# Seven matmuls of the identity by itself ahead of the first product of a two-layer encoder trunk

## Chip, cores and metric

One core of a Trainium2 chip runs the whole program. The metric is the device time of one execution in microseconds (us), as the median of several runs.

## What is computed

The reference is a trunk of two post-norm layers over 256 tokens of width 2048, in float32. Each layer is a mixer and a SwiGLU feed-forward block, each followed by a residual layer norm:

```python
for layer in range(DEPTH):
    if layer % 2 == 0:
        y = ab_mixer(x, ab_w_in[j], ab_w_out[j], na_rpb[j], lower_bounds[j], hg_norm_w[j])
    else:
        y = cd_mixer(x, cd_w_in[j], cd_w_out[j], pool_w[j], pool_scale[j], d_q_norm[j], d_k_norm[j], cos, sin)
    x = layer_norm(DN_ALPHA * x + y, ln_mix_g[layer], ln_mix_b[layer])
    f = swiglu(x, ffn_w_gate[layer], ffn_w_up[layer], ffn_w_down[layer])
    x = layer_norm(DN_ALPHA * x + f, ln_ffn_g[layer], ln_ffn_b[layer])
```

The mixer of the first layer begins with one input projection, `proj = x @ w_in`, of 256 x 2048 by 2048 x 8192. Its first 512 columns are the first products of the program.

## The kernel before

The kernel is written with a scheduling layer: the Python code issues tiles and instructions, and a scheduler with a time model of its own sets the order of each engine's queue, except where `tc.keep_in_program_order` pins an instruction.

Every large product is made three times. A float32 operand is split into a rounded part and the rest: `split` (lines 126 to 128) has ScalarE (ACT) copy the source into `hi`, and VectorE (DVE) subtract `hi` from the source into `lo`. `mm3` (line 286) then issues three matmuls into one accumulator: activation rest by weight `hi`, activation `hi` by weight `hi`, activation `hi` by weight rest. In the rows these are `acc<-whi,xTl`, `acc<-whi,xTh` and `acc<-wlo,xTh`. This text calls each such matmul of 128 x 128 by 128 x 512 a product.

Weights come in halves. `load_half` (line 152) loads 256 rows by 512 columns (512 KB) into `raw` through SP's queue and splits them into `whi` and `wlo`, which live in a ring of six buffers in the first mixer. One half serves twelve products: two slices of 128 rows, two tiles of 128 tokens, three matmuls. `mm_chunk` (line 191) takes the eight halves of a chunk of 512 output columns. In the first chunk `load_x` (line 608) also loads and splits the transposed input, four slices at a time for every second half, and the first half and the first input are loaded in two pieces each, so that the first products can start early. Half 0 and half 1 therefore serve products 1 to 24, and half 2 begins with product 25.

The identity matrix `ident` (lines 110 and 111) is made on GpSimd (POOL) at the very start: a memset and an affine select. Its users are the transposes (line 124), the first of them after the first chunk. PSUM tiles come from rings of banks: `acc()` has three, `trp()` (tiles named `tr`) two, `mxp()` three.

At the end of `trunk`, lines 989 to 994 make the tiles for the input and call the first mixer, which issues the first product. Nothing stands for TensorE (PE) ahead of it.

Of the kernel before, what the change touches and what calls it, by code (L numbers as in the profile page):

```python
# [18 lines left out]
P = 128  # L19
# [15 lines left out]
RMS_EPS = 1e-6  # L35
QSCALE = 128 ** -0.5
FILL = -3.0e38


A_Q, A_K, A_V, H_Q, H_FF, H_FB, H_I, H_G = (8 * i for i in range(8))  # L40
# [40 lines left out]
def trunk(ctx: ExitStack, tc: tile.TileContext, a, out):  # L81
    nc = tc.nc
# [16 lines left out]
    def bank(tag, bufs):  # L99
        return banks["pool"].tile([P, NCH], F32, tag=tag, name=tag, bufs=bufs)  # L100

    def side_bank(other=False):
        return bank("ab"[banks["side"] ^ other] + "side", 4)
# [6 lines left out]
    ident = cp.tile([P, P], F32, name="ident")  # L110
# [6 lines left out]
    def trp():  # L117
        return bank("tr", 2) if banks["kind"] == "uses" else side_bank(True)
# [131 lines left out]
    def new_xT():  # L250
        xh = [ap_.tile([P, KT, P], F32R, tag=f"xTh{t}", name=f"xTh{t}") for t in range(NT)]
        xl = [ap_.tile([P, KT, P], F32R, tag=f"xTl{t}", name=f"xTl{t}") for t in range(NT)]
        return xh, xl

    def new_yT():
        yh = ap_.tile([P, 4, T], F32R, tag="yTh", name="yTh", bufs=4)
        yl = ap_.tile([P, 4, T], F32R, tag="yTl", name="yTl", bufs=4)
        return yh, yl
# [348 lines left out]
    def ab_mixer(mp, xT, yT):  # L607
# [196 lines left out]
        def natten(i, outs):  # L804
# [15 lines left out]
            for h in range(2):  # L820
# [6 lines left out]
                for qt in range(NT):  # L827
# [4 lines left out]
                        scale=1.0,  # L832
                        scalar=FILL,
                        op0=add,
# [151 lines left out]
                pool(kind[1], outs)  # L986


    xT = new_xT()
    yT = [new_yT() for _ in range(4)]  # L990
    with tc.tile_pool(name="wab", bufs=1) as wab:
# [41 lines left out]
def constants():  # L1033
# [5 lines left out]
    inside = (col[None, :] >= start[:, None]) & (col[None, :] < start[:, None] + NA_COLS)  # L1039
    colmask = np.tile(np.where(inside, 0.0, FILL), (2, 1)).astype(np.float32)  # L1040
    pos = np.arange(T)
# [83 lines left out]
def build(nc, arrays):  # L1125
    args = {}
    for name, v in arrays.items():
        t = nc.dram_tensor(name, v.shape, mybir.dt.from_np(v.dtype), kind="ExternalInput")
        args[name[3:]] = t.ap()
    out = nc.dram_tensor("out", (T, D), F32, kind="ExternalOutput").ap()  # L1130
    with tile.TileContext(nc, schedule_with_timeline_sim=True) as tc:
        trunk(tc, args, out)
# [11 lines left out]
```

## Time and profile before

| | us |
|---|---|
| median of 3 runs | 2211.68 (2210.59 to 2213.93) |
| the profiled execution's own time | 2208.31 |
| its span, first to last instruction | 2206.5 |
| PE busy | 2176.5 (99% of the span) |
| DVE busy | 1564.1 (71%) |
| ACT busy | 1053.2 (48%) |
| POOL busy | 42.2 (2%) |

The span is the time from the first to the last instruction; 1.8 us of the profiled execution lie outside it. The profiled execution is one of its own, and shorter than the three timed runs. A matmul's shown duration is longer than its share of PE's time, since matmuls are pipelined: the time from one start to the next is what one costs in a dense stretch. A timeline merges equal instructions that follow each other into one row with a count.

### The profile page before, as it was taken

Reading aid. Unit: us, or ns where it says so; the run is one execution under the profiler, and the core shown is the slowest. Engines: PE = TensorE matmul, PEld = TensorE weight load, DVE = VectorE, ACT = ScalarE, POOL = GpSimd, SP = SyncE. Lnnn points to the kernel's source line nnn. Section 1 sums busy time; section 2 is a strip of 40 time slices with the busy share of each in tenths; the row PEclk is TensorE's granted clock in tenths of the full one; section 3 lists DMA queues with packets and bytes.
Section 4 is the critical chain, followed back from the end, with each engine's and each line's share of the span. In section 5 each row is a group of like instructions: output and inputs, shape, how many; then the busy total and the mean of one; then the engine's idle time right before and its main releaser. Section 6 shows DMA issues by size and latency. Waiting matters only on the chain. (4 is left out here: it accounts for less than half of the span.)

```text
span 2206.5 us, 26606 instructions
## 1 busy us (share of the span) xinstructions
PE 2176.5 (99%) x10048; PEld 1806.2 (82%) x10048; DVE 1564.1 (71%) x1960; ACT 1053.2 (48%) x1276; POOL 42.2 (2%) x43
## 2 busy tenths in 40 slices
PE   8999999999999999999999989999999999999997
PEld 7888888888888888888888778888888878888886
DVE  6886688567538787577877676677357886668865
ACT  6445544546435445445544554555344554445442
POOL 0000001000000000000000000000000000000001
PEclk9999999999999999999999999999999999999999
DMA  8555546684636565565557363657456555655573
GB/s 288 163 163 180 171 126 191 210 276 141 231 117 240 178 206 186 190 228 185 189 180 269 127 206 124 213 169 237 154 172 225 184 180 194 212 198 183 179 249 114
DMA packets 112562, 420.64 MB, mean 191 GB/s; under 512 B 13744, under 2 KB 16304, under 8 KB 105520
## 3 DMA queue, kind: packets, MB, share of 16 engines
q1 hardware_dynamic: 112432, 418.93, 57.0%
q8 instruction: 79, 1.29, 0.2%
q14 instruction: 51, 0.42, 0.1%
HBM read 416.78 MB, written 2.10 MB: 190 GB/s over the span
## 5 line engine op out<-in xcount | busy, mean ns | idle before, releaser
L128 DVE TENSOR_TENSOR wlo<-raw,whi 128x1024 fp32r<-128x1024 f32 (+1 forms) x673 | 818.8, 1224 | 435.2 <-ACT whi L127 425.0
L127 ACT CAST whi<-raw 128x1024 fp32r<-128x1024 f32 (+1 forms) x673 | 704.8, 1052 | 827.3 <-PE acc L290 329.0
L290 PE MATMUL acc<-whi,xTl 128*128 128x512 f32 x1056 | 418.3, 397 | 13.2 <-DVE rx L889 6.5
L290 PE MATMUL acc<-whi,xTh 128*128 128x512 f32 x1056 | 415.3, 393 | 0.0
L290 PE MATMUL acc<-wlo,xTh 128*128 128x512 f32 x1056 | 412.7, 393 | 1.0 <-DVE wlo L128 1.0
L290 PEld LDWEIGHTS acc<-whi,xTl 128*128 128x128 f32 x1056 | 199.8, 189 | 54.2 <-ACT whi L127 8.2
L290 PEld LDWEIGHTS acc<-wlo,xTh 128*128 128x128 f32 x1056 | 199.5, 189 | 42.6 <-DVE wlo L128 1.9
L290 PEld LDWEIGHTS acc<-whi,xTh 128*128 128x128 f32 x1056 | 199.8, 189 | 39.2
L290 PE MATMUL acc<-whi,yTl 128*128 128x512 f32 x512 | 200.4, 392 | 0.1
L290 PE MATMUL acc<-whi,yTh 128*128 128x512 f32 x512 | 199.5, 390 | 0.0
L290 PE MATMUL acc<-wlo,yTh 128*128 128x512 f32 x512 | 197.7, 390 | 0.0
L290 PE MATMUL aside<-whi,xTl 128*128 128x512 f32 x336 | 131.2, 390 | 0.4 <-ACT g L480 0.4
L290 PE MATMUL bside<-whi,xTl 128*128 128x512 f32 x336 | 131.2, 390 | 0.1
L290 PE MATMUL bside<-whi,xTh 128*128 128x512 f32 x336 | 131.0, 390 | 0.0
L290 PE MATMUL aside<-whi,xTh 128*128 128x512 f32 x336 | 131.0, 390 | 0.0
L290 PE MATMUL bside<-wlo,xTh 128*128 128x512 f32 x336 | 128.2, 390 | 0.0
L290 PE MATMUL aside<-wlo,xTh 128*128 128x512 f32 x336 | 128.1, 390 | 0.0
L290 PEld LDWEIGHTS acc<-wlo,yTh 128*128 128x128 f32 x512 | 96.1, 188 | 20.4 <-DVE wlo L128 0.5
L290 PEld LDWEIGHTS acc<-whi,yTl 128*128 128x128 f32 x512 | 96.1, 188 | 19.9 <-DVE yTl L973 0.3
L290 PEld LDWEIGHTS acc<-whi,yTh 128*128 128x128 f32 x512 | 96.2, 188 | 19.3
L128 DVE TENSOR_TENSOR sl<-z,sh 128x2048 fp32r<-128x2048 f32 x44 | 100.7, 2289 | 6.2 <-ACT sh L127 5.6
L439 ACT CAST sh<-rs 128x1536 fp32r<-128x1536 f32 x44 | 65.2, 1483 | 74.7 <-DMA rs<-in_gu 32.9
(257 smaller groups left out, 3109.5 us busy)
## 6 DMA issues: line engine op xcount, KB each, us to landing
raw<-in_gu SPq DMA_DIRECT2D x264, 512.0 KB, 4.7
raw<-in_down SPq DMA_DIRECT2D x176, 512.0 KB, 3.6
raw<-in_ab_in SPq DMA_DIRECT2D x127, 512.0 KB, 4.1
rs<-in_gu SPq DMA_DIRECT2D x44, 1024.0 KB, 5.8
raw<-in_cd_in SPq DMA_DIRECT2D x40, 512.0 KB, 4.1
raw<-in_ab_out SPq DMA_DIRECT2D x32, 512.0 KB, 4.4
raw<-in_cd_out SPq DMA_DIRECT2D x32, 512.0 KB, 4.4
x<-in_xT SPq DMA_DIRECT2D x8, 256.0 KB, 6.4
```

Of the source, the lines that this page charges most:

```text
L127: nc.scalar.copy(hi, src)
L128: return nc.vector.tensor_tensor(lo, src, hi.bitcast(F32), op=sub).ins
L290: ins = nc.tensor.matmul(o, lhs[a], rhs[b], start=start and n == 0, stop=stop and n == 2)
L439: nc.scalar.copy(hi[:, :3], raw[:, :3])
```

## The change

Seven matmuls with `ident` as both operands are issued into the first 128 columns of a `tr` bank, before the input's tiles are made. They are pinned in program order, and nothing reads the result. Lines behind the new constant move by one, and those behind the loop by five.

```diff
 FILL = -3.0e38
+WARM = 7
...
+    idle = trp()
+    for _ in range(WARM):
+        tc.keep_in_program_order(nc.tensor.matmul(idle[:, :P], ident, ident, start=True, stop=True))
     xT = new_xT()
     yT = [new_yT() for _ in range(4)]
     with tc.tile_pool(name="wab", bufs=1) as wab:
```

The scheduler's order of PE's queue at the start of the program, before (`tr` is the PSUM tile, `xTl` and `xTh` the split input, `whi` and `wlo` the split weights):

```order
L1131 UNCONDITIONAL_BRANCH
L290 MATMUL acc<-whi,xTl_79 128x512
L290 MATMUL acc<-whi,xTh_77 128x512
L290 MATMUL acc<-wlo,xTh_77 128x512
L290 MATMUL acc<-whi,xTl_79 128x512
```

The same place now:

```order
L1136 UNCONDITIONAL_BRANCH
L993 MATMUL tr<-ident 128x128 x7
L291 MATMUL acc<-whi,xTl_87 128x512
L291 MATMUL acc<-whi,xTh_85 128x512
L291 MATMUL acc<-wlo,xTh_85 128x512
L291 MATMUL acc<-whi,xTl_87 128x512
```

The seven stand at the head of PE's queue, and the products follow in the order that they had.

The order of ACT's queue in the second chunk, where the first head group's gates are computed (`sg`, `kf` and `kb` are sigmoids of the transposed projection), before:

```order
L680 ACTIVATE kf<-tr 128x512
L127 CAST whi<-raw 128x1024 x2
L678 ACTIVATE sg<-tr 128x512
L680 ACTIVATE kb<-tr 128x512
L127 CAST whi<-raw 128x1024 x4
```

The same place now:

```order
L681 ACTIVATE kf<-tr 128x512
L128 CAST whi<-raw 128x1024
L679 ACTIVATE sg<-tr 128x512
L681 ACTIVATE kb<-tr 128x512
L128 CAST whi<-raw 128x1024 x5
```

One cast of a weight half has moved behind two sigmoids. The DVE subtractions that belong to such casts move behind five or six short operations of the same gates there, and on PE one product moves behind six transposes. On all engines the rest stands as it stood.

## Rows read from the trace of the kernel before

**Rows 1.** The page: the span, and each engine's busy time.

```profile
span 2206.5 us, 26606 instructions
PE 2176.5 (99%) x10048; PEld 1806.2 (82%) x10048; DVE 1564.1 (71%) x1960; ACT 1053.2 (48%) x1276; POOL 42.2 (2%) x43
```

**Rows 2.** PE's waits over the whole span: total us, times, longest us.

```profile
PE acc L290 <- DVE rx L889: 6.5, 1, 6.5
PE acc L290 <- DVE xTl L128: 5.5, 1, 5.5
```

**Rows 3.** Timeline of the start: start us, us, instruction, count [idle before <-releaser].

```profile
1.94 0.29 POOL masks.py:199 TENSOR_SCALAR_AFFINE_SELECT ident<-ident 128x128 f32<-128x128 f32 x1
...
5.46 0.77 PE L290 MATMUL acc<-whi,xTl 128*128 128x512 f32 x1 [5.46 <-DVE xTl L128]
...
6.45 0.63 PE L290 MATMUL acc<-wlo,xTh 128*128 128x512 f32 x1
7.18 0.62 ACT L127 CAST whi<-raw 128x512 fp32r<-128x512 f32 x1 [1.16 <-DMA raw<-in_ab_in]
...
7.85 0.79 PE L290 MATMUL acc<-whi,xTl 128*128 128x512 f32 x1 [0.77 <-ACT whi L127]
...
8.44 0.63 PE L290 MATMUL acc<-whi,xTh 128*128 128x512 f32 x1
...
8.87 0.63 PE L290 MATMUL acc<-whi,xTl 128*128 128x512 f32 x1
...
9.50 1.23 DVE L128 TENSOR_TENSOR wlo<-raw,whi 128x1024 fp32r<-128x1024 f32 x1 [0.98 <-ACT whi L127]
...
11.54 1.04 ACT L127 CAST whi<-raw 128x1024 fp32r<-128x1024 f32 x1 [0.63 <-DMA raw<-in_ab_in]
...
12.61 2.50 DVE L128 TENSOR_TENSOR wlo<-raw,whi 128x1024 fp32r<-128x1024 f32 x2 [0.69 <-ACT whi L127]
12.68 0.39 PE L290 MATMUL acc<-whi,xTl 128*128 128x512 f32 x1
...
12.91 0.39 PE L290 MATMUL acc<-whi,xTh 128*128 128x512 f32 x1
...
14.97 0.39 PE L290 MATMUL acc<-whi,xTl 128*128 128x512 f32 x1
...
15.88 0.39 PE L290 MATMUL acc<-wlo,xTh 128*128 128x512 f32 x1
```

**Rows 4.** Windows at the start: length, busy (count) by engine, granted clock, DMA.

```profile
5.46:12.45 6.99, 6.22 (x14) 4.43 (x15) 4.30 (x6) 4.37 (x6) 0.00 (x0) 1.00 1.01 375
...
5.46:14.97 9.51, 8.74 (x24) 6.47 (x25) 6.61 (x8) 6.59 (x9) 0.00 (x0) 1.00 1.02 386
```

**Rows 5.** Windows around the stall in the second layer's mixer, columns as before.

```profile
1270.90:1275.00 4.10, 0.17 (x1) 0.00 (x0) 0.69 (x4) 0.10 (x1) 0.00 (x0) 1.00 0.86 245
...
1275.40:1275.80 0.40, 0.00 (x0) 0.00 (x0) 0.00 (x0) 0.37 (x3) 0.00 (x0) 0.71 0.89 348
...
1277.60:1282.00 4.40, 4.40 (x11) 3.43 (x12) 4.03 (x12) 1.61 (x5) 1.21 (x2) 0.50 0.32 120
...
1282.20:1282.40 0.20, 0.20 (x1) 0.11 (x1) 0.18 (x1) 0.00 (x0) 0.00 (x0) 0.52 0.00 0
```

**Rows 6.** Plain float32 matmuls of 128 x 128: the tile's row, then timeline.

```profile
L713 PE MATMUL mx<-qq,kk x256: 270/275/275, 68.1 to 365.8; 128*128 128x128 f32 x128
...
68.13 1.05 PE L713 MATMUL mx<-qq,kk 128*128 128x128 f32 x8
68.94 0.48 PE L290 MATMUL acc<-whi,xTl 128*128 128x512 f32 x1
```

**Rows 7.** Groups of ACT from 0 to 42.3 us, and of PE to 42.36.

```profile
L127 ACT CAST whi<-raw 128x1024 fp32r<-128x1024 f32 (+1 forms) x18 | 17.9, 1005 | 8.3 <-DMA raw<-in_ab_in 8.0 <-PE acc L290 0.2
...
L290 PE MATMUL acc<-whi,xTl 128*128 128x512 f32 x47 | 20.0, 425 | 6.2 <-DVE xTl L128 5.5 <-ACT whi L127 0.8
```

## Prediction

> **What bounds the kernel now.** I read the page first: PE is busy for 99% of a span of 2206.5 us [rows 1]. So time is won or lost where PE waits or runs slowly, and hardly elsewhere. PE's waits come next. Two long ones hold nearly all of its idle time: 5.5 us at the very start, until DVE has split the first input, and 6.5 us once in the second layer's mixer [rows 2]. The change touches the first.
>
> The timeline of the start shows how PE gets going [rows 3]. Product 1 starts at 5.46 and product 3 at 6.45; PE then stands idle for 0.77 us, because the second piece of half 0 is cast only from 7.18 to 7.80, and product 4 starts at 7.85. From there on PE is dense. What the reader is to see is the distance between starts: 8.44 to 8.87 is 0.43 us, but 12.68 to 12.91 is 0.23, and 14.97 to 15.88, four products, is 0.2275 each. The products are the same; only the clock differs. 512 columns in 0.43 us is 1.2 GHz, in 0.23 us close to 2.4 GHz. The granted clock in the windows shows 1.00 for this stretch [rows 4]; the later stall tells why I trust the distances more. There the same products run at a granted 0.50, 11 of them in 4.40 us, 0.40 each [rows 5], which is the rate of the start. So PE ran at 1.2 GHz until about 12.45, and its first 14 products were slow [rows 4].
>
> The windows around the later stall also show when the level changes [rows 5]. PE stops near 1271.1, the granted clock stays at 1.00 for over 4 us and falls at about 1275.5. PE resumes at 1277.6 (7 us after the stop), and the clock is back at about 1282.4, 4.8 us later. At the start the rise came 7.0 us after product 1, with the break of 0.77 us in between. Idle PE lost the full clock, working PE got it back.
>
> **The change, part by part.** It adds seven float32 matmuls of 128 x 128 at the head of PE's queue. It removes nothing, and no transfer is added or moved.
>
> *What the seven cost.* They need only the identity, whose last POOL instruction ends at 1.94 + 0.29 = 2.23 [rows 3]; with a hand-over of 0.05 to 0.2 us they start at about 2.4, where PE is idle. A plain float32 matmul shows as two rows: L713 has 256 rows in all for 128 instructions (four head pairs, eight levels, four matmuls), and eight rows take 68.94 - 68.13 = 0.81 us, 0.10 each [rows 6]. At the slow clock that doubles to 0.20. Seven matmuls are 14 rows, 2.8 to 3.0 us, so they end at 5.2 to 5.4, just before product 1 can start. If they ran a little over, products 1 to 3 would slip into the idle 0.77 us ahead of product 4, which waits for a cast and not for PE. The cost is therefore nothing up to an end at 6.2; behind that, every microsecond counts. The upper bound is a row at its whole shown length, 0.275 us [rows 6], doubled and not overlapped: 14 x 0.55 = 7.7 us, an end at 10.1. I take the dense value, since those rows are the same kind of instruction back to back.
>
> *What the clock gives.* With PE at work from 2.4, I move the two observed delays there. With 4.8 us the clock is up at 7.2, with 7.0 us at 9.4.
> - Up at 7.2: products 4 to 24 take 21 x 0.2275 = 4.8 us from 7.85, so product 25 comes at 12.63. No data stops them: the rest of half 1 is there at 9.50 + 1.23 = 10.73, and product 17, its first user, comes at 10.8. Product 25 needs the cast of half 2, which ends at 12.58, just in time. Product 29 is the first to use the rest of half 2, ready at 12.61 + 1.25 = 13.86 (the first of the two subtractions); it would come at 13.54 and so waits until 13.9. Before it came at 15.88 [rows 3]. The gain is 2.0 us.
> - Up at 9.4: products 4 to 7 are slow (7.85, 8.44, 8.87, 9.29), product 8 comes at about 9.6, product 25 at 13.5 and product 29 at 14.4. The gain is 1.5 us.
>
> I take 1.9: the seven and products 1 to 3 run without a break from 2.4 to 6.9, which is nearer to the restart at 1277.6 than to the broken start. The bounds are 0, if the seven do not count, and 2.0, where the data stop PE. Even an ideal start could not give more than about 14 x (0.43 - 0.2275) = 2.8 us on these products.
>
> Here a rule of the Trainium skill speaks against the change. TensorE: Matmul & The Clock Gate says in What's actually happening that the slow clock is the default and activity releases it; the rows agree (1282.4 and 12.45). But its Part 4 says of transposes on TensorE that the full clock does not engage for that mode, since they don't count as PE being busy in the same way. The seven look like transposes of the identity but are issued as plain matmuls; if that rule held for them, the sum would be 0 instead of 1.9. No run here shows it yet. The same section says that the number of slow matmuls at a kernel's start varies from run to run.
>
> *Does the gain reach the end?* The wait of 6.5 us in the second layer hangs on work that PE's own products feed, so it moves with PE, and all other waits of PE are short. In the first chunk the casts and transfers run ahead of PE; later they are released by PE and move forward with it. So I carry 1.9 us through.
>
> *The moved cast.* ACT now runs one weight cast behind two sigmoids (0.6 us each), and DVE's subtractions there slip by some short operations. By 42.3 us 18 casts had begun, two of them of half size, so 17 halves, while PE had begun 3 x 47 = 141 products, less than 12 halves [rows 7]. The moved cast is of the 17th half, whose first product is number 193: 51 products away, 51 x 0.2275 = 11.6 us. A slip of 1.2 us on ACT, and of a few on DVE, is covered; it would cost only what exceeds that. I cost it at nothing, and likewise the product that moves behind six transposes, since the transposes' input was long there.
>
> *Sum.* -1.9 us: 2208.31 - 1.9 = 2206.4 for the profiled execution. That execution lies 3.4 us below the median of the runs, so against the runs I set 2211.68 - 1.9 = 2209.8. It is 0.09% of the time. A measurement of this kernel can tell about 0.2%, 4.4 us, from no change.
>
> **The rivals.**
> 1. *The seven don't count.* PE's clock rises only for the products, as before. For it: all but the diagonal of the operands is zero, unlike in any product of the rows. Against it: they are plain matmuls, of the form that the mixer uses in the middle of dense stretches at full rate. Time unchanged: 2211.7.
> 2. *The seven are drawn out.* If their rows don't overlap, they end at 10.1, product 1 starts 4.6 us late, and even with the full clock 24 products take 5.5 us and product 25 comes at 15.6 instead of 14.97: 0.6 us slower, 2212.3. If the clock then also rises only 7.0 us after product 1, at 17.1, there are 16 slow products and 8 fast ones, product 25 comes at 18.9, 3.9 us late: 2215.6. It turns from gain to loss where the seven end later than 14.97 - 24 x 0.2275 = 9.5, half a microsecond a row. Against it: eight such rows take 0.81 us [rows 6], and the start has nothing else on PE.
> 3. *The gain is spent at the later stall.* The delay of the rise after PE resumes differs: 4.8 us there, 7.0 at the start. The stall now comes earlier by the gain; should the rise need 7.0 us there, 2.2 us more run at half speed and 1.1 us are lost. 0.8 us remain: 2210.9. Nothing in the rows says which way it would turn.
>
> **How the numbers follow.** My forecast, a gain of 1.5 to 2.0 us, has a chance of 0.66; the first rival 0.17, the second 0.06, the third 0.11. All of them but the slow end of the second lie within 0.2%. What can carry the result beyond it is the scatter of executions: three runs span 3.3 us, and the profiled one lies 2.3 us below the lowest. The low end is the forecast less that scatter, 2209.8 - 3.3 = 2206.5. The high end takes in the first rival, the second's lower price and some of the scatter: 2213.0. Faster by over 0.2% would take 2.5 us of luck on top of the gain, 0.07; slower by over 0.2% takes the second rival's slow end or scatter, 0.04; within 0.2% is 0.89.
>
> **What would show it.** Right: 14 rows of the new line on PE from about 2.4 to 5.4; product 1 within 0.5 us of 5.46; product 4 at 7.85, still waiting for the cast; starts 0.23 us apart by product 8; product 29 at 13.9 to 14.4 with a short wait for DVE; the last product some 1.9 us earlier, 2 us less span. Starts 0.43 us apart until 11 us or later would show the first rival; a first product behind 9.5 the second; a granted 0.50 for longer than 4.8 us after the later stall the third. I would be wrong if the order's small moves open a wait of PE near 42 to 60 us, or if the time changes by more than 3 us in either direction.

## The result, and the profile after

The changed kernel takes 2214.9 us (median of 22 runs, 2209.85 to 2220.96), the kernel before 2211.05 on the same chip (22 runs, 2208.58 to 2214.65). The ratio is 1.0019, 95% interval 1.0011 to 1.0026: 4.2 us slower (2.4 to 5.8), where 1.9 us less was forecast. Medians and ratios leave out two single executions that were far slower than all others, 4474.2 us in e2_banks below and 5582.74 us in the kernel before.

The profiled execution took 2215.33 us, its span is 2213.6. The page of the changed kernel, against [rows 1]:

```profile
span 2213.6 us, 26632 instructions
PE 2181.7 (99%) x10062; PEld 1809.5 (82%) x10062; DVE 1562.4 (71%) x1960; ACT 1052.5 (48%) x1276; POOL 42.1 (2%) x43
```

PE has 14 matmul rows more, as forecast, and is busy for 5.2 us more. The longest of its waits over the span, against [rows 2] (total us, times, longest us):

```profile
PE acc L291 <- DVE rx L890: 6.6, 1, 6.6
PE tr L125 <- DVE sil L517: 3.6, 2, 2.8
PE aside L291 <- DVE yTl L129: 2.5, 2, 1.9
PE tr L993 <- POOL ident masks.py:199: 2.3, 1, 2.3
```

The wait of 5.5 us at the start has become one of 2.3. But two waits have grown that [rows 2] were too small to show: for `sil`, and of the first `aside` products for `yTl`. The kernel before has these two as follows:

```profile
PE tr L124 <- DVE sil L516: 1.3, 2, 0.8
PE aside L290 <- DVE yTl L128: 0.5, 1, 0.5
```

The timeline of the start of the changed kernel, against [rows 3] (start us, us, instruction, count, idle before and releaser):

```profile
2.28 3.36 PE L993 MATMUL tr<-ident 128*128 128x128 f32 x14 [2.28 <-POOL ident masks.py:199]
...
5.45 0.80 PE L291 MATMUL acc<-whi,xTl 128*128 128x512 f32 x1
...
6.45 0.62 ACT L128 CAST whi<-raw 128x512 fp32r<-128x512 f32 x1 [0.41 <-DMA raw<-in_ab_in]
...
7.12 0.50 PE L291 MATMUL acc<-whi,xTl 128*128 128x512 f32 x1
...
7.46 0.40 PE L291 MATMUL acc<-whi,xTh 128*128 128x512 f32 x1
...
7.69 0.40 PE L291 MATMUL acc<-whi,xTl 128*128 128x512 f32 x1
...
13.80 0.50 PE L291 MATMUL acc<-wlo,xTh 128*128 128x512 f32 x1
```

The 14 rows start from 2.28 on, and product 1 follows at 5.45, 3.2 us later. From product 5 on, at 7.46, starts lie 0.23 us apart: the full clock. Product 4 comes at 7.12 and not at 7.85, because the cast that it waits for begins at 6.45 in this execution and at 7.18 in [rows 3]. Product 29, the last row, starts at 13.80 instead of 15.88. So in this pair of profiles the start gains what the prediction says, and the loss came later.

To find where, I subtract the start of each PE instruction in the first profile of before from that of the same instruction in another trace. The changed kernel is 2.1 us ahead at product 29 and still 1.85 ahead at 645 us. At 660 it is 0.13 us behind, at 1500 2.0 behind, at 1545 7.0, and so it stays to the end. Two stretches carry most of it: **645 to 660** (2.0 us) and **1500 to 1545** (5.0 us). From 660 to 1260 the changed kernel falls back by another 2.1 us, but this is not the change's doing: nine of the twelve traces taken later lose 2.5 to 4.2 us there against the first profile of before, and the second profile of before is one of them, with 3.2.

### The profile page after: what moved, and what is told of

The parts are those of the page before. It is cut to its first block, busy times and chain, and to the rows that moved or that the text cites. A ratio compares the mean times of both kernels' runs of the same rounds, so it can differ in the third digit from the quotient of the medians.

```text
span 2213.6 us, 26632 instructions
## 1 busy us (share of the span) xinstructions
PE 2181.7 (99%) x10062; PEld 1809.5 (82%) x10062; DVE 1562.4 (71%) x1960; ACT 1052.5 (48%) x1276; POOL 42.1 (2%) x43
```

## What stands at 650 us: banks

Near 650 us the first layer's feed-forward block turns from its first gate and up products to the first down product (the loads change from `in_gu` to `in_down`), and the program opens another PSUM pool: `acc`, `tr` and `mx` give way to the two rings of four banks `aside` and `bside`. PE's and DVE's timeline there in the kernel before (`yTl<-tr` is DVE's copy out of the transposes' banks):

```profile
648.77 1.38 PE L124 MATMUL tr<-ident,sil 128*128 128x128 f32 x8
649.91 0.47 PE L290 MATMUL aside<-whi,yTl 128*128 128x512 f32 x1
...
650.75 1.28 DVE L128 TENSOR_TENSOR yTl<-tr,yTh 128x512 fp32r<-128x512 f32 x2
```

PE begins the `aside` products 0.84 us before DVE begins to read `tr`. In the changed kernel (the first row shows the last five of eight transposes):

```profile
647.31 1.00 PE L125 MATMUL tr<-ident,sil 128*128 128x128 f32 x5
...
648.90 1.28 DVE L129 TENSOR_TENSOR yTl<-tr,yTh 128x512 fp32r<-128x512 f32 x2
...
650.24 0.50 PE L291 MATMUL aside<-whi,yTl 128*128 128x512 f32 x1 [1.93 <-DVE yTl L129]
```

DVE is 1.85 us ahead of before, but PE's product now waits 1.93 us until the copies end at 650.18. The reason stands in the program, not in the order of the queues; the traces don't show bank numbers, and the experiments below test it. A pool gives banks to its tags in the order of their first use. Before, `acc` was first (banks 0 to 2), then `tr` (3 and 4), then `mx` (5 to 7). `idle = trp()` makes `tr` the first tag: `tr` gets 0 and 1, `acc` 2 to 4. The next pool gives `aside` the banks 0 to 3, and its first product takes bank 0, which now is one that DVE still reads.

That gave the first theory (A): the tag costs, not the matmuls. The other theories of the first four runs were that the seven or the moved cast cost time themselves (B), that the late losses are scatter (C), and that a fall of the clock near 1530 us belongs to the change (D).

## The experiments

All times are medians, with ratios to the kernel before on the same chip. The runs after the first pair came in four groups on four chips; before took 2210.85 us beside e1 to e4, 2210.91 beside e5 to e8, 2211.91 beside e9 to e11 and 2209.01 beside e12: across groups, compare the ratios. Rows are the matmul and weight-load rows that stand ahead of the first product. The last four columns come from each kernel's profile: by how much product 29 starts later than in the first profile of before, what the stretch 645 to 660 us adds to that difference, how long the load of `in_gu` near 1493 us takes to land, and what the stretch 1500 to 1545 us adds.

| kernel | first tag | rows | us | ratio, 95% interval | product 29 | 645-660 | load | 1500-1545 |
|---|---|---|---|---|---|---|---|---|
| before | acc | 0 | 2211.05 | 1 | 0 | 0 | 3.74 | 0 |
| changed | tr | 28 | 2214.9 | 1.0019 (1.0011, 1.0026) | -2.08 | +1.98 | 5.98 | +4.96 |
| e1_acc | acc | 28 | 2211.07 | 1.0002 (0.9992, 1.0012) | -1.53 | +0.01 | 4.61 | +0.43 |
| e2_banks | tr | 4 | 2212.79 | 1.0014 (1.0001, 1.0027) | -1.61 | +3.56 | 3.70 | -0.02 |
| e3_after_again | tr | 28 | 2213.75 | 1.0019 (1.0007, 1.0030) | -1.68 | +3.59 | 5.62 | +3.00 |
| e4_before_again | acc | 0 | 2210.24 | 0.9995 (0.9987, 1.0004) | -0.92 | 0.00 | 3.68 | +1.06 |
| e5_wide | acc | 8 | 2208.23 | 0.9982 (0.9972, 0.9992) | -1.63 | 0.00 | 3.69 | +0.19 |
| e6_tiny | acc | 28 | 2211.22 | 1.0003 (0.9994, 1.0012) | -0.79 | +0.01 | 4.28 | +0.42 |
| e7_both | acc | 64 | 2211.72 | 1.0005 (0.9997, 1.0014) | -1.63 | +0.02 | 3.73 | -0.29 |
| e8_acc_again | acc | 28 | 2210.96 | 1.0001 (0.9992, 1.0010) | -2.15 | +0.01 | 4.50 | +0.80 |
| e9_wide_again | acc | 8 | 2211.84 | 1.0002 (0.9988, 1.0015) | -2.08 | +0.02 | 3.64 | -0.08 |
| e10_wide_rows | acc | 28 | 2210.95 | 1.0005 (0.9994, 1.0016) | -0.56 | +0.02 | 5.62 | +2.31 |
| e11_wide_tr | tr | 8 | 2212.98 | 1.0013 (1.0002, 1.0024) | -1.86 | +3.55 | 3.70 | +0.40 |
| e12_sides | tr | 28 | 2211.59 | 1.0009 (1.0000, 1.0018) | -1.71 | -0.25 | 4.75 | +0.02 |

### The tag alone, the matmuls alone, and both kernels again

e1_acc takes the idle tile from `acc`, so that the banks stand as before:

```diff
-    idle = trp()
+    idle = acc()
```

> The seven matmuls write into a bank of acc() instead of trp(), so the banks of PSUM are dealt out as before the change (acc 0 to 2, tr 3 and 4), while the seven and the order of all queues are those of the changed kernel. Theory A (the tr bank taken first gives the first side banks of the feed-forward block to the transposes' tiles, and PE waits at 650 us until DVE has read them): the gain of 1.9 us at the start stays, no wait of 1.9 us for yTl at 650, so 1.5 to 2 us faster than before, about 2209. Theory B (the seven matmuls or the moved cast cost the time, wherever the banks are): as slow as the changed kernel, 2 to 4 us slower than before, about 2214.

e2_banks keeps the `tr` tile and all but drops the matmuls:

```diff
-WARM = 7
+WARM = 1
```

> [...] Theory A: no gain at the start, a wait of PE of about 2 us for yTl near 652 us, so 2 us slower than before at that place, about 2213. Theory B: within 1 us of before, 2211.

e3_after_again and e4_before_again are the changed kernel and the one before, unedited.

> The changed kernel once more, for a second profile. Theory A alone gives a gain of 1.9 us at the start and a loss of 2 us at 650, so the time of before within 0.5 us; the first measurement had 3.9 us more. Theory C (behind 650 us the two programs are the same, and what differs there is the scatter of transfers and of the clock's dips): this profile has not the wait of 2.8 us for sil near 1528 us nor a granted 0.50 there. Theory D (the dip near 1530 us comes from the change): it has both.

> The kernel before once more, as a control and for a second profile. Theory C: its stretch from 653 us to the end scatters by 2 to 4 us against the first profile, as the changed kernel's does. Theory D: it scatters by under 1 us, and the changed kernel's is longer each time.

The tag carries it. With the seven but the old banks the kernel is level with before (1.0002); with one matmul and the new banks it is slower (1.0014). Against its expectation e2_banks also gained at the start, 1.61 us at product 29, so even that is no baseline for the clock. The stretch 645 to 660 follows the tag in every row of the table but e12_sides, where the next pool is changed too. It adds 2.0 us in one trace with `tr` first and 3.6 in the three others. The 1.6 us between come from the clock. Windows of e11_wide_tr around the wait (length, busy by engine with counts, granted clock, DMA share, GB/s):

```profile
650.00:651.50 1.50, 1.29 (x4) 1.05 (x5) 0.15 (x1) 0.00 (x0) 0.00 (x0) 0.71 0.90 265
651.50:655.00 3.50, 3.50 (x12) 2.75 (x11) 0.00 (x0) 0.38 (x1) 0.00 (x0) 0.64 0.09 36
```

PE is busy throughout the second window, yet at a granted 0.64, a mix of 1.2 and 2.4 GHz: here the clock fell right behind a wait of 1.9 us, with eight transpose rows just ahead of the wait. The changed kernel's own profile has 1.00 there:

```profile
650.00:652.00 2.00, 1.76 (x8) 1.46 (x9) 0.18 (x1) 0.00 (x0) 0.00 (x0) 1.00 0.80 252
652.00:656.00 4.00, 4.00 (x19) 3.33 (x18) 1.83 (x2) 1.26 (x2) 0.00 (x0) 1.00 0.00 1
```

Theory B falls as a cause of the slowdown: e1_acc has the seven and the moved cast, and is not slower. Of C, e4_before_again shows how large scatter is: the unchanged kernel's second profile is 6.1 us behind its first at the end, after being 1.2 us ahead at 660, with no single cause; that is more than C expected. So one profile prices a stretch only where several agree. D holds in part: near 1530 us the granted clock is below 1.00 in both profiles of the changed kernel (0.61 over 1530 to 1538 below, 0.79 in e3_after_again), and 1.00 over 1524 to 1545 in e1_acc, e2_banks and e4_before_again.

### Only the banks, in the other direction

e12_sides leaves the changed kernel as it is, up to the place where the pool of the sides is opened. There it names the tag `bside` first, so that `aside` gets the banks 4 to 7. The order of every queue stays that of the changed kernel.

```diff
-                open_banks("sides")
+                open_banks("sides"); [bank("bside", 4) for _ in range(4)]
```

> The changed kernel (seven matmuls, idle tile from tr) with one edit at the place where the pool of the sides is opened: the tag bside is named first, so that bside takes the banks 0 to 3 and aside the banks 4 to 7, and the first products after the switch no longer lie on the two banks of tr (0 and 1). The order of every engine's instructions is that of the changed kernel. Theory A (what costs is the first aside product on a bank that DVE still reads): the stretch 645 to 660 goes back to within 0.3 us of before from the 2.0 to 3.6 us of the kernels with tr first; time 2 to 4 us below the changed kernel, so within 1 us of before (2210 to 2212). Rival (something else of the tag tr costs there, or the wait moves to the banks of acc or mx): the stretch keeps 1.5 us or more, time 2213 to 2216.

The stretch goes from +1.98 to -0.25, as theory A expected. The time bears this out only in part: the ratio goes from 1.0019 to 1.0009 (1.0000 to 1.0018), so the kernel is still 2.0 us above before, not within 1 us of it. The median of 2211.59 lies in the expected range of absolute times only because before takes 2209.01 us on this chip. PE's and DVE's timeline there:

```profile
647.93 0.48 PE L291 MATMUL aside<-whi,yTl 128*128 128x512 f32 x1
...
648.77 1.28 DVE L129 TENSOR_TENSOR yTl<-tr,yTh 128x512 fp32r<-128x512 f32 x2
```

PE again starts 0.84 us ahead of the copy, as before the change. A transpose, a copy and a product that are the same and in the same order wait or don't wait by the bank alone: theory A is shown for the wait at 650 us. The edit also holds for the second layer, where `tr` has the banks 3 and 4 and `aside` now begins at 4. There the same wait opens in mirror image, on the first `aside` product:

```profile
1613.15 0.65 PE L291 MATMUL aside<-whi,yTl 128*128 128x512 f32 x1 [1.34 <-DVE yTl L129]
```

In the kernel before, the first `aside` product starts straight behind the transposes, and only a later one waits, for less:

```profile
1611.79 0.47 PE L290 MATMUL aside<-whi,yTl 128*128 128x512 f32 x1
...
1613.97 0.51 PE L290 MATMUL aside<-whi,yTl 128*128 128x512 f32 x1 [0.55 <-DVE yTl L128]
```

So this edit gives back part of what it saves (its stretch 1545 to 1760 adds 2.4 us, 0.0 in the others), and 1.0009 is not quite 1.

### Why the gain at the start does not show

With the old banks the seven should still be worth their gain; e1_acc shows none. In the changed kernel a load of `in_gu` issued at 1494.79 lands late. The DMA view of the changed kernel from its issue to its landing, and of the issue alone (median us to landing last):

```profile
q8 instruction: 1, 0.02, 2.3%
...
raw<-in_gu SPq DMA_DIRECT2D x1, 512.0 KB, 6.0
```

The same load in the kernel before, whose view from issue to landing has no such packet:

```profile
raw<-in_gu SPq DMA_DIRECT2D x1, 512.0 KB, 3.7
```

The q8 packets of kind instruction carry 16 KB each, 79 in the span, some 28 us apart. Counted along PE's program, that is less what PE is behind the first profile of before at that place, they come some 3 us earlier in kernels with 28 rows more (the last one of the changed kernel at 2191.80 less 7.03, which is 2184.8, against 2187.7). In the changed kernel that puts one, from 1496.40 for 2.24 us, on this load; before, it came at 1500.67, after the landing. PE then waits for `sil` near 1530, in windows of the changed kernel:

```profile
1526.00:1530.00 4.00, 1.39 (x7) 0.81 (x5) 2.87 (x3) 1.82 (x3) 0.00 (x0) 0.92 0.96 336
1530.00:1538.00 8.00, 7.77 (x26) 6.53 (x27) 4.76 (x7) 3.55 (x5) 0.00 (x0) 0.61 0.49 166
```

The same places before, with PE busy throughout at full clock:

```profile
1526.00:1530.00 4.00, 4.00 (x22) 3.28 (x23) 3.34 (x5) 2.50 (x4) 0.00 (x0) 1.00 0.81 263
1530.00:1538.00 8.00, 8.00 (x37) 6.64 (x36) 5.18 (x5) 3.95 (x4) 0.00 (x0) 1.00 0.75 252
```

`sil` comes late because of its place in DVE's order, behind the subtraction of a weight half. In the changed kernel:

```profile
1528.36 1.23 DVE L129 TENSOR_TENSOR wlo<-raw,whi 128x1024 fp32r<-128x1024 f32 x1 [1.09 <-ACT whi L128]
1529.50 0.68 DVE L517 TENSOR_TENSOR sil<-sil,acc 128x512 f32<-128x512 f32 x1
```

PE's products are done by 1527.4, where its wait of 2.8 us begins, but DVE stands 1.09 us for ACT's cast of that half, and the casts ahead of it stand for loads of `in_gu` (1.40 us before 1524.96) or for earlier subtractions (1.27 us before 1527.28). So this wait hangs on the stream of loads, not on one load alone: e4_before_again, whose load lands after 3.68 us, waits 1.6 us there. What the wait costs also hangs on the clock. e10_wide_rows (below) waits 2.8 us too, but its granted clock stays at 1.00 and its stretch adds 2.31 us instead of 4.96:

```profile
1530.00:1538.00 8.00, 6.80 (x34) 5.62 (x35) 7.14 (x9) 5.39 (x6) 0.00 (x0) 1.00 0.70 244
```

Theory F says that these displaced packets take the gain back, theory G that the gain is lost at later waits whatever they do. Four runs varied rows and columns apart.

e5_wide, the same columns in 8 rows:

```diff
-    idle = trp()
-    for _ in range(WARM):
-        tc.keep_in_program_order(nc.tensor.matmul(idle[:, :P], ident, ident, start=True, stop=True))
+    idle = acc().rearrange("p (n t) -> p n t", n=4)
+    eye = ident.rearrange("p (n t) -> p n t", n=1)
+    for n in (4, 3):
+        tc.keep_in_program_order(nc.tensor.matmul(idle[:, :n], ident, eye.to_broadcast([P, n, P]), start=True, stop=True))
```

> Edit: the idle tile comes from the acc tag, so the banks stand as before the change, and the seven matmuls of 128 columns become two, of 512 and 384 columns: the same 896 columns of the identity, in 8 instead of 28 matmul and weight-load rows. What is asked of this call: with the banks as before, the seven gained 1.5 to 2 us at the start and yet ended at no gain; who took it back? Theory F (fetch): the trace shows packets of kind instruction, 16 KB each, some 79 of them about 28 us apart; counted along PE's program they come some 3 us earlier with the seven, and the one near 1496 to 1500 then lies on the load of in_gu issued near 1493, which lands after 4.6 to 6.0 us instead of 3.7, and PE stands for it at 1500 to 1545. By F two wide matmuls move the fetches by under 1 us: start up to 16 us 1.3 to 2.0 us ahead of before, load of in_gu landing in 3.7 to 4.2 us, stretch 1500 to 1545 within 0.5 us of before, time 1.0 to 2.0 us below before (2208.5 to 2209.5). Theory G (the gain of the start is lost at later waits whatever the fetches do): start as by F, but time within 0.7 us of before and of the acc run of this call. Theory H (one matmul of 512 columns does not keep TensorE as busy as four of 128): the clock goes up 2 us or more later than at 7.4, and the start gains under 1 us.

e6_tiny, 28 rows with hardly any columns:

```diff
-    idle = trp()
+    idle = acc()
     for _ in range(WARM):
-        tc.keep_in_program_order(nc.tensor.matmul(idle[:, :P], ident, ident, start=True, stop=True))
+        tc.keep_in_program_order(nc.tensor.matmul(idle[:8, :8], mhalf, mhalf, start=True, stop=True))
```

> Edit: idle tile from the acc tag, and the seven matmuls are of 8 by 8 on the small constant mhalf instead of 128 by 128 on the identity: 28 rows on PE as in the change, hardly any columns. Theory F (fetch): no earlier clock, start within 0.5 us of before; the instruction packets along PE's program 3 us earlier as in the change, the one near 1496 on the load of in_gu, which lands after 4.6 to 6 us; time 1.5 to 3 us above before (2212 to 2213.5). Theory G (gain of the start lost later whatever the fetches do): without a gain nothing is lost, time within 0.7 us of before.

e7_both, 64 rows:

```diff
-    idle = trp()
+    idle = acc()
+    for _ in range(9):
+        tc.keep_in_program_order(nc.tensor.matmul(idle[:8, :8], mhalf, mhalf, start=True, stop=True))
```

> Edit: idle tile from the acc tag, nine tiny matmuls of 8 by 8 on mhalf ahead of the seven of the identity: 64 rows on PE, so by theory F the instruction packets come some 7 us earlier along PE's program than before the change, and the one of this place near 1488 to 1491, ahead of the issue of the load of in_gu at 1493. Theory F: the load lands in 3.7 to 4.2 us, the stretch 1500 to 1545 is within 0.5 us of before, start 1.3 to 2.0 us ahead, time 0.5 to 2 us below before; other places where a packet then meets a load are possible and would show as a late load of their own. Theory G: time within 0.7 us of before.

e8_acc_again, the program of e1_acc:

```diff
-    idle = trp()
+    idle = acc()
```

> The changed kernel with the idle tile from the acc tag once more, the same program as the first run with this edit, so that the three others have it beside them on the same chip. Both theories: within 0.7 us of before (2210.5 to 2212); F: the load of in_gu issued near 1493 again lands after more than 4.2 us, with an instruction packet inside it.

The landing went by F each time: 4.28 us or more with 28 rows, 3.7 with 8 and with 64. The times did not. e6_tiny should have been 1.5 to 3 us slower and was level; e7_both should have been faster and was not. Only e5_wide came out faster, by more than F allowed. So the late landing is real, but F's price for it was wrong. G fits e6_tiny and e8_acc_again, and nearly e7_both, but not this result of e5_wide. H is out: e5_wide has the full clock by 8.14 us and gains 1.63 at product 29. Three more runs asked whether e5_wide was luck (theory S) or the rows (theory R), and tried the tag once more.

e9_wide_again is e5_wide unedited. e10_wide_rows puts five tiny matmuls ahead of the two wide ones:

```diff
-    idle = acc().rearrange("p (n t) -> p n t", n=4)
+    warm = acc()
+    for _ in range(5):
+        tc.keep_in_program_order(nc.tensor.matmul(warm[:8, :8], mhalf, mhalf, start=True, stop=True))
+    idle = warm.rearrange("p (n t) -> p n t", n=4)
```

e11_wide_tr is e5_wide with the tile from `tr`:

```diff
-    idle = acc().rearrange("p (n t) -> p n t", n=4)
+    idle = trp().rearrange("p (n t) -> p n t", n=4)
```

> The two wide matmuls (512 and 384 columns, idle tile from the acc tag) once more, the same program as the first run of them, which took 2208.2 against 2210.9 us before. Theory R (the extra rows of the seven are what takes their gain back, by the earlier instruction packets or otherwise): 1.6 to 3.6 us below before again. Theory S (the first result was partly luck of the run): 0.5 to 1.6 us below before, the gain of the start and no more, or less. The load of in_gu issued near 1493 to 1496 lands in 3.6 to 3.9 us by either.

> The two wide matmuls with five tiny ones of 8 by 8 on mhalf ahead of them: the columns of the identity and the start as in the wide run, but 28 rows on PE as with the seven. Theory R: as the seven in the acc tag, within 0.7 us of before and 1.5 to 3.5 us above the wide run of this call, and the load of in_gu lands after 4.2 to 6 us with an instruction packet inside it. Theory S: as the wide run of this call within 0.7 us, whenever that load lands.

> The two wide matmuls with the idle tile from the tr tag, as in the change: the only difference to the wide run of this call is the tag that is used first, so the banks. Theory A (the tag costs 2 us at the switch of the banks near 650 us, and up to 1.6 us more where the clock falls there): 2 to 4 us above the wide run of this call, so 0.5 us below to 1.5 us above before; PE waits 1.9 us for the copy out of tr in the stretch 645 to 660. Rival (the tag costs only together with the seven, as when the load of in_gu is late): as the wide run of this call within 0.7 us.

e9_wide_again is level with before (1.0002): the same program that gave 0.9982. The second result lies outside the first one's interval, so the 2.7 us of e5_wide are not established, and no version here is shown to beat before. e10_wide_rows is as fast as e9_wide_again within the uncertainty, although its load lands late, with the packet on it. The view of e10_wide_rows from issue to landing, and of the issue alone:

```profile
q8 instruction: 1, 0.02, 1.0%
...
raw<-in_gu SPq DMA_DIRECT2D x1, 512.0 KB, 5.6
```

R is right on the landing and not borne out in the time; S stands. e10_wide_rows also missed the start that both theories expected: its clock rose late, and product 29 gained only 0.56 us. e11_wide_tr has the wait and the late clock in the stretch 645 to 660 (+3.55) and 1.0013: 1.1 us above e9_wide_again by the medians and 2.4 by the ratios, where 2 to 4 were expected, and on the same side as the three other kernels with `tr` first.

## Why the prediction was wrong

**The failed step** is the sentence "all other waits of PE are short ... So I carry 1.9 us through", with what stood ahead of it, that on all engines the rest stands as it stood. That is true of the order of the queues, and I took it for the whole program. The change also takes a tile, and the tile's tag decides the banks of a whole pool. At the next change of pools it puts PE's first product on a bank that DVE reads. No view of the trace of before shows the coming wait, but the two pieces were there: `trp()` as first user in the diff, and PE starting `aside` 0.84 us before DVE's copy out of `tr`. The four kernels with `tr` first and nothing done about it add 1.98, 3.56, 3.59 and 3.55 us at 645 to 660, 3.2 on the mean; the other ten -0.25 to 0.02. The times agree without any profile: the ratios of these four average 1.0016, those of the seven kernels with matmuls ahead and `acc` first 1.0000, a difference of 3.6 us.

**The seven's cost, nothing: right.** They start at 2.28 (2.4 forecast), and product 1 starts at 5.45, no later than before. The second rival, rows that don't overlap, is out: 14 rows take 3.2 us.

**The clock's gain: mechanism right, size too large.** The clock is up by product 5, 7.46 (7.2 forecast), product 29 starts at 13.80 (13.9 forecast). That the two agree so closely is partly luck: product 4 came 0.73 us before its place in the forecast, with the early cast, and products 13 and 17 then came only at 9.61 and 10.87. The first rival is out: starts 0.23 to 0.24 us apart begin at 8.29 us at the latest in nine of the ten profiles with 896 columns of the identity ahead, and at 9.92, 11.28, 11.68 and 12.68 us in the four without (e2, e4, e6 and the first of before). The rule of the Trainium skill that was weighed there (TensorE: Matmul & The Clock Gate, Part 4, that the full clock does not engage for transposes) does not reach plain matmuls of the identity in this trace: 14 such rows from 2.28, full clock by 7.46. But 1.9 us was worked out against one execution. The three others without the seven, with at most one matmul of the identity by itself, reach product 29 at -0.92 (e4), -0.79 (e6) and -1.61 us (e2) against it; with the first one's 0 the mean is -0.83. The ten with 896 columns of the identity average -1.69. So the gain is 0.9 us on the mean. It isn't sure either: in e10_wide_rows, with the columns done, products still lay 0.43 us apart from 8.52 to 10.66 us and product 29 gained 0.56 us only.

**The moved cast, nothing: right.** The difference at 40 us is -1.93, at 560 -1.90.

**The third rival, loss at the later stall: not in the first profile, but in the second.** From 1260 to 1300 the changed kernel gains 0.5 us. Behind the wait of 6.6 us its products run slowly for a while, as in [rows 5]; a window of the changed kernel there:

```profile
1279.60:1284.00 4.40, 4.20 (x11) 3.38 (x12) 3.84 (x13) 1.80 (x6) 1.45 (x2) 0.54 0.38 143
```

In e3_after_again, the same program, the starts stay 0.43 us apart for 5.7 us behind the stall, longer than the 4.8 that the prediction named as the sign, and the stretch adds 0.6 us:

```profile
1283.06 0.77 PE L291 MATMUL acc<-whi,xTl 128*128 128x512 f32 x1 [6.60 <-DVE rx L890]
...
1288.31 0.63 PE L291 MATMUL acc<-whi,xTl 128*128 128x512 f32 x1
1288.74 0.46 PE L291 MATMUL acc<-whi,xTh 128*128 128x512 f32 x1
```

Over the 14 profiles the stretch adds between -0.95 and 0.6 us, so as far as these profiles tell it is scatter from one execution to the next and no cost of the change. (The prediction's 7 us from PE's stop to its restart are 6.5 by [rows 2]; nothing hangs on it.)

**What was not thought of at all:** that more instructions on PE move its instruction packets onto other transfers. From issue to landing the load takes 4.28 to 5.98 us in all seven kernels with 28 rows, 3.64 to 3.74 in the seven others, so this effect is shown. Its price isn't: the stretch 1500 to 1545 adds 1.7 us on the mean of the seven and 0.2 on that of the others, but e1_acc, e6_tiny, e8_acc_again and e10_wide_rows, which all have it, are at 1.0001 to 1.0005. Within the seven the price goes with the delay: 2.3 to 5.0 us in the three profiles with a landing of 5.6 us or more, 0.0 to 0.8 in the four with 4.75 or less.

As an estimate from these means, 3.2 us for the banks, 1.5 for the load and 0.9 less at the start give 3.8 us, against 4.2 (2.4 to 5.8) measured. The banks are shown by edits in both directions, the other two only read from profiles. What stays open: how much of PE's wait for `sil` is due to the packets and how much to the scatter of the other loads, whether that or mere scatter hides the gain of the start in e1_acc and e8_acc_again, and why e5_wide and e9_wide_again, one program on two chips, lie 3.6 us apart. A gain of 0.9 us is 0.04% and below what these runs can tell.

## What to carry to other kernels

A change that "only adds" still takes a buffer. Ask which tag it uses first, what that does to the banks of its pool, and who still reads those banks where the next pool opens; a comparison of the queues' order does not show it. Before a gain of 2 us is carried to the end of a kernel of 2.2 ms, look whether a second execution of the same program starts at the same time: here they differed by 0.9 us at product 29 and by 6.1 at the end.

## What the runs showed of the hardware

- Packets of kind instruction stand among the data in the profile of the 16 DMA engines: 16 KB, 0.88 to 2.42 us each near 1500 us, and one on the load of 512 KB near 1493 us goes with 0.5 to 2.3 us of delay in its landing. With 28 more rows on PE they come some 3 us earlier along its program, with 64 some 7.
- Behind a wait of PE of 1.9 us, with eight transpose rows just ahead of it, the clock was lower in three of four profiles (granted 0.64 over 651.5 to 655.0 in e11_wide_tr), and not in the fourth.
- Without the seven, and with one or none of the identity's matmuls ahead, the clock's first rise is not a fixed point of the program: at about 12.5 us in the first profile of before, but product starts are 0.24 us apart from 11.68 us in e6_tiny.
